# HGRN2 diagonal and levels of 1 to 16 tokens as column-tiled products in chunks of 32, and 512-column value projections

## The chip, the cores and the metric

The kernel runs on one core of a Trainium2 chip. The core has a matrix engine (TensorE, "PE" in the profile, with its weight loads listed apart as "PEld"), an elementwise engine (VectorE, "DVE"), an activation engine (ScalarE, "ACT"), a general engine (GpSimd, "POOL") and a queue engine (SyncE, "SP") that starts transfers. SBUF is the on-chip memory; PSUM, into which TensorE writes, has eight banks, each of 512 fp32 numbers for each of 128 partitions. The metric is the device time of one execution in microseconds, as the median over runs.

## The reference

One decoder layer over 512 tokens of width 1024, in fp32. A single projection of x gives the inputs of two token mixers. The first is an mLSTM with 4 heads of 512. The second is HGRN2 with 8 heads, key width 128 and value width 128. Both results are normalised, gated, projected and merged; two layer norms and a SwiGLU network follow. The part around the change is HGRN2, here for one head, with log_f the log of a forget gate, k = 1 - f and chunks of 16 tokens:

```python
a = jnp.cumsum(lfc, axis=2)
rel = jnp.where(causal, a[:, :, :, None, :] - a[:, :, None, :, :], -jnp.inf)
scores = jnp.einsum('bhtk,bhtsk,bhsk->bhts', qc, jnp.exp(rel), kc)
o = (jnp.einsum('bhts,bhsv->bhtv', scores, vc)
     + jnp.einsum('bhtk,bhkv->bhtv', qc * jnp.exp(a), state))
```

The score of query token t and key token s is a sum over 128 features of q, k and the product of all forget gates between s and t. The values vc are a plain projection, x times columns of W_in plus a bias; so are the values of the mLSTM.

## The kernel before

**Products.** Every large product is done by `mm3` (lines 83 to 86): both operands are split in a rounded high part and a remainder (`split`, line 89: a cast on ScalarE and a subtraction on VectorE), and three matmuls add high x high, high x low and low x high into one PSUM bank. HGRN2's own products multiply plain fp32 operands; the trace shows each of these as two weight loads and two matmuls.

**Weights.** `fetch` brings 512 KB of a weight matrix into one of five raw buffers (`wraw`, started on SP's queue) and splits it into one of three pairs `whi` and `wlo`. `proj_sub` (line 141) makes a projection with features in the partitions: 128 weight columns are stationary and 512 tokens move, 8 x 3 matmuls of 512 columns. `natural_proj` (line 156) makes one with tokens in the partitions: a 128 x 128 block of x is stationary and weight columns move, 256 at a time. It makes 4 token tiles x 8 x 3 = 96 matmuls of 256 columns, with one fetch for each half of the contraction, into two PSUM banks with two token tiles in each.

**Order.** `tick()` is called after each projection; `defer(n, fn)` puts a piece of other work behind n further ticks (half steps exist). So the attention, the HGRN2 levels and the norms are laid between projections. A planner of the framework then orders each engine's instructions by its own costs, keeping to priorities and dependencies.

**mLSTM stage.** Four heads in turn. Each has eight feature projections (keys, queries), then two value projections of 256 columns (`natural_proj` and `values`; the first head has one of its halves done ahead, with the gates), then four output gates. `attend` multiplies weights and values; a column of ones beside the first 256 value columns gives the denominator. PSUM holds three `pp` banks for projections, three score banks and two `px` banks.

**HGRN2 stage.** Four pairs of heads. `h_units` (line 527) makes for each pair the projections f (two; they give the gates and K), Q (two), the values (one `natural_proj` with the bias load `vb`), and the output gates (two): eight ticks. `h_chain` (line 721) then lays the pair's scores into the ticks of the next pair's projections, for the last pair into those of the merge gates. PSUM holds three `pp` and five `px` banks.

The scores are built up by levels. A tile `ad` holds, for both heads and four blocks of 128 tokens, the scores inside a block.

- The diagonal and the levels of 1 and 2 tokens go a direct way (`h_direct_0` to `h_direct_3`). VectorE multiplies K and Q element by element (`h_terms`, 128 x 512, five times for a pair), the product is split, and a matmul with a matrix of ones as the stationary operand sums it over the 128 features (`h_sum`, line 579, two matmuls of 512 columns each, ten for a pair). A predicated copy with a mask puts the sums in place in `ad`.
- A level of hs tokens (`h_level`, line 637) multiplies K of the first half of each group of 2 hs tokens with Q of the second half. Between levels `h_advance` (lines 592, 593, 596) multiplies the gates into K and Q, so each level's products come after the advance of the level before.
- Levels 4 and 8 (line 656) take whole blocks: 128 stationary columns of K, 64 moving columns of Q, eight products for a pair. Only a part of what they give is used; `h_place` (line 604) picks it with a mask from 512 columns.
- Levels 16 and 32 (line 647) take only the groups. With `tile_position=(0, s0)` a product uses a strip of the array's columns, s0 being 0, 32, 64 or 96 for level 16 (32 products of 16 stationary and 16 moving columns) and 0 or 64 for level 32 (16 products of 32 and 32).
- Levels 64, 128 and 256 (lines 661, 667, 673) follow, and `h_out` (line 689) multiplies the scores with the values and normalises.

The direct steps are due after 0, 1, 2 and 3 ticks, the levels after 3.5, 4, 4.5, 5, 5.5, 6 and 6.5, the outputs after 7 and 7.5.

Of the kernel before, what the change touches and what calls it, by code (L numbers as in the profile page):

```python
# [15 lines left out]
P = 128  # L16
# [20 lines left out]
def tile_hybrid_trunk(  # L37
# [79 lines left out]
    ones_r = cst.tile([P, P], FR, name="ones")  # L117
    ones = ones_r.bitcast(F32)
# [30 lines left out]
    def natural_half(outs, s_, wh, wl, shared=True):  # L149
        for t in range(NT):  # L150
            for k in range(4):
                kx = 4 * s_ + k
                mm3(outs[t], xh[:, kx, t * P:(t + 1) * P], xl[:, kx, t * P:(t + 1) * P], wh[:, k], wl[:, k],
                    kx == 0 and not (shared and t % 2), kx == KD - 1, skip_group_check=True)

    def natural_proj(off):
        vps = [psum(pp, "pp", (P, 2, 256)) for _ in range(2)]
        outs = [vps[t // 2][:, t % 2] for t in range(NT)]
        for s_ in range(2):
            natural_half(outs, s_, *fetch(win[s_ * 512:(s_ + 1) * 512, off:off + 256], 4, 256))  # L160
            if s_ == 0:
                tick()
        return vps
# [57 lines left out]
    for s_ in range(2):  # L221
        natural_half(vps0, s_, *wv[s_], shared=False)
# [156 lines left out]
    def values(h, u2, vps, vt_):  # L379
        vh, vl, vb = vt_  # L380
        us2 = slice(u2 * 256, (u2 + 1) * 256)
        vs2 = slice(u2 * 258, u2 * 258 + 256)
        for g in range(2):
            vt = mp.tile([P, 2, 256], F32, tag="w32", name="vt", bufs=4)
            nc.vector.tensor_add(vt, vps[g], vb[:, None, us2].to_broadcast([P, 2, 256]))
            split(vt, vh[:, 2 * g:2 * g + 2, vs2], vl[:, 2 * g:2 * g + 2, vs2])

    def value_tiles(h):
        vh = mp.tile([P, NT, 514], FR, tag="vh", name="vh")
        vl = mp.tile([P, NT, 514], FR, tag="vl", name="vl")  # L390
        nc.vector.memset(vh[:, :, 256:258].bitcast(F32), 1.0)
        nc.vector.memset(vl[:, :, 256:258].bitcast(F32), 0.0)
        vb = mp.tile([P, MD], F32, tag="vb", name="vb")
        nc.sync.dma_start(vb, b_in[:, O_MV + h * MD:O_MV + (h + 1) * MD].to_broadcast([P, MD]))
        return vh, vl, vb

    def attend(h, tiles, wth, wtl, vh, vl, hn):
        for i in tiles:
            nps = [psum(px, "px", (P, 258)), psum(sp, f"s{i % 3}", (P, 256))]
            for e, vs in enumerate((slice(0, 258), slice(258, 514))):  # L400
# [3 lines left out]
            den = nps[0][:, 256:257]  # L404
# [50 lines left out]
    for h in range(MH):  # L455
# [57 lines left out]
    for key, gs_, w in (((1, 0), 2, 1), ((2, 0), 4, 2), ((2, 1), 4, 2), (4, 8, 4), (8, 16, 8)):  # L513
        a, n = (key[1], 1) if isinstance(key, tuple) else (0, w)
        m = hp_.tile([P, P // gs_, w], F32, name=f"mask{gs_}{a}")
        nc.gpsimd.memset(m, 1.0)
        for sg_, base in ((1, -a), (-1, a + n - 1)):
            nc.gpsimd.affine_select(m, m, pattern=[[-gs_ * sg_, P // gs_], [0, w]],
                                    compare_op=OP.is_ge, fill=0.0, base=base, channel_multiplier=sg_)
        masks[key] = m  # L520
    ads = []
    for i in range(2):
        ad = hp_.tile([P, 8, P], F32, name=f"ad{i}")
        nc.gpsimd.memset(ad, 0.0)
        ads.append(ad)

    def h_units(pr):

        st = dict(pr=pr, ad=ads[pr % 2])
        for name in ("f", "K", "Q", "og"):  # L530
            st[name] = hp_.tile([P, 2, T], F32, tag=name, name=name, bufs=2)
        st["v"] = hp_.tile([P, NT, 256], F32, tag="v", name="v", bufs=2)
        st["tot"] = hp_.tile([P, 1024], F32, tag="tot", name="tot", bufs=1)
        f, K, Q, og, v = (st[k] for k in ("f", "K", "Q", "og", "v"))
# [17 lines left out]
        vb = hp_.tile([P, 256], F32, tag="vb", name="vb")  # L552
        nc.sync.dma_start(vb, b_in[:, O_HI + pr * 256:O_HI + (pr + 1) * 256].to_broadcast([P, 256]))
        vps = natural_proj(O_HI + pr * 256)
        for g in range(2):
            nc.vector.tensor_add(v[:, 2 * g:2 * g + 2], vps[g], vb[:, None, :].to_broadcast([P, 2, 256]))
        tick()
# [7 lines left out]

    def h_terms(in0, in1, shape):

        e = hp_.tile(shape, F32, tag="e", name="e", bufs=2)
        eh = hp_.tile(shape, FR, tag="eh", name="eh", bufs=2)
        el = hp_.tile(shape, FR, tag="el", name="el", bufs=2)  # L570
        nc.vector.tensor_mul(e, in0, in1)
        split(e, eh, el)
        return eh, el

    def h_sum(parts, n):

        ps = psum(px, "px", (P, T // n, n))
        for i, part in enumerate(parts):
            nc.tensor.matmul(ps.rearrange("p j n -> p (j n)"), ones_r, part.rearrange("p a b -> p (a b)"),  # L579
                             start=(i == 0), stop=(i == 1))  # L580
        return ps
# [18 lines left out]
    def h_place(st, ps, gs_, w, key):  # L600

        dst = st["ad"].rearrange("p j (g k) -> p j g k", k=gs_)[:, :, :, gs_ - w:]
        msk = masks[key].bitcast(U32)[:, None].to_broadcast([P, 8, P // gs_, w])
        nc.vector.copy_predicated(dst, msk, ps.rearrange("p j (g k) -> p j g k", k=w))

    def h_direct_0(st):
        K, Q, f = st["K"], st["Q"], st["f"]
        st["e"] = [h_terms(K[:, c:c + 1], Q[:, c:c + 1], [P, 1, T]) for c in range(2)]
        nc.vector.tensor_mul(Q, Q, f)
        st["cur"] = f.rearrange("p c t -> p (c t)")  # L610
# [4 lines left out]
    def h_direct_1(st):  # L615
        ad = st["ad"]
        dpss = [h_sum(parts, P) for parts in st["e"]]
        qv, kv = h_halves(st, 1)
        st["e"] = h_terms(kv[:, :, 0], qv[:, :, 1], [P, T, 1])
        h_advance(st, 1)  # L620
        for c in range(2):
            nc.vector.copy_predicated(ad[:, 4 * c:4 * c + 4], ident.bitcast(U32)[:, None, :].to_broadcast([P, NT, P]),
                                      dpss[c])

    def h_direct_2(st):
        ps = h_sum(st["e"], 64)
        qv, kv = h_halves(st, 2)
        st["e"] = [h_terms(kv[:, :, 0, a:a + 1].to_broadcast([P, 256, 2]), qv[:, :, 1], [P, 256, 2]) for a in range(2)]
        h_advance(st, 2)
        h_place(st, ps, 2, 1, (1, 0))  # L630

    def h_direct_3(st):
        pss = [h_sum(parts, 64) for parts in st["e"]]
        for a in range(2):
            h_place(st, pss[a], 4, 2, (2, a))

    def h_level(st, hs):

        K, Q, ad = st["K"], st["Q"], st["ad"]
        if hs in (16, 32):  # L640

            lps = psum(px, "px", (P, 8, 64))
            for c in range(2):
                for j in range(NT):
                    for g in range(64 // hs):
                        s0 = 2 * hs * g
                        nc.tensor.matmul(lps[s0:s0 + hs, 4 * c + j, hs * g:hs * (g + 1)],
                                         K[:, c, j * P + s0:j * P + s0 + hs], Q[:, c, j * P + s0 + hs:j * P + s0 + 2 * hs],
                                         start=True, stop=True, tile_position=(0, s0))
        elif hs < 64:  # L650
            lps = psum(px, "px", (P, 8, 64))
            for c in range(2):
                for j in range(NT):
                    js = slice(j * P, (j + 1) * P)
                    mov = Q[:, c, js].rearrange("p (g two h) -> p g two h", two=2, h=hs)[:, :, 1]
                    nc.tensor.matmul(lps[:, 4 * c + j], K[:, c, js], mov, start=True, stop=True)  # L656
# [21 lines left out]
        if hs < 16:  # L678
            h_place(st, lps, 2 * hs, hs, hs)
        elif hs < 64:  # L680
            for g in range(64 // hs):
                rows_ = slice(2 * hs * g, 2 * hs * g + hs)
                nc.scalar.copy(ad[rows_, :, 2 * hs * g + hs:2 * hs * (g + 1)], lps[rows_, :, hs * g:hs * (g + 1)])
# [5 lines left out]
    def h_out(st, c):  # L689
# [3 lines left out]
        vc = lambda j: st["v"][:, j, c * P:(c + 1) * P]  # L693
# [47 lines left out]
    sgb2 = [hp_.tile([P, 2, T], F32, tag=tag, name="sgb", bufs=2) for tag in ("f", "K", "Q", "v")]  # L741
# [184 lines left out]
```

## Time and profile before

| | |
|---|---|
| median of 3 runs (lowest, highest) | 1326.18 us (1325.97, 1326.56) |
| profiled execution, its own time | 1324.7 us |
| its span, first to last instruction | 1322.9 us |
| mean granted TensorE clock | 0.997 |
| stretch of the span read for the HGRN2 stage | 548 to 820 us |
| bytes moved, share of 16 transfer engines | 141.34 MB, 37.1% |

The page lists busy times, slices, queues, the chain of work that ended last, the costliest groups and the transfers. In the timeline a row has the start and the length in us, the engine, the line of the kernel, the operation, "out<-in" by tile names, stationary rows * columns and the moving operand's size, and xcount. Lengths of matmuls overlap, since the array is a pipeline. In the view of groups the two numbers after the bar are the busy time in us and the mean of one in ns. In the view of stretches a row has the stretch, its length, and for each engine the busy us and the number of instructions: TensorE, weight loads, VectorE, ScalarE, GpSimd; at the end stand the granted clock, the share of the transfer engines and GB/s. With a filter such a row has only the engine asked for; instructions still running from before are counted too.

### The profile page before, as it was taken

The page shows a single profiled execution, that of the slowest core. Times are in us where ns is not written, and L with a number is a line of the kernel's source. Part 1 is how long each engine was busy: PE and PEld are TensorE (multiplying, and loading weights), DVE is VectorE, ACT ScalarE, POOL GpSimd, SP SyncE. Part 2 cuts the span into 40 slices and gives each one's busy share as a digit, 9 for nine tenths or more (in the row PEclk, how much of TensorE's full clock was granted, in tenths as well). Part 3 has the DMA queues.
Part 4 walks back from the last instruction along what each step waited for, and adds up shares of the span by engine and source line. Part 5 has one row for each costly group of instructions (what it writes and reads, how often), then busy time and mean ns, then how long its engine had stood idle before and what let it go on. Part 6 is the DMA issues. An engine that isn't in the chain of part 4 may idle for free.

```text
span 1322.9 us, 17916 instructions
## 1 busy us (share of the span) xinstructions
PE 1306.4 (99%) x7279; PEld 1124.9 (85%) x7279; DVE 752.2 (57%) x1140; ACT 536.4 (41%) x811; POOL 41.1 (3%) x78
## 2 busy tenths in 40 slices
PE   8999999999999999999999999999999999999997
PEld 7788889888988898889898988887898888888885
DVE  5774656466556654458686764255765433334565
ACT  5764553444343533323434333333773222223332
POOL 0000000000000001000000000000000000000001
PEclk9999999999999999999999999999999999999999
DMA  8322333223322323333232322336664343335672
GB/s 236 80 72 80 91 86 90 78 80 96 88 80 80 96 80 84 96 84 84 64 85 65 79 64 65 96 95 204 200 180 127 97 132 96 96 96 168 195 225 81
DMA packets 189426, 141.34 MB, mean 107 GB/s; under 512 B 5728, under 2 KB 178592, under 8 KB 189344
## 3 DMA queue, kind: packets, MB, share of 16 engines
q1 hardware_dynamic: 188288, 140.17, 37.1%
q8 instruction: 57, 0.93, 0.3%
q14 instruction: 25, 0.20, 0.1%
q10 hardware_dynamic: 1056, 0.03, 0.0%
HBM read 138.09 MB, written 2.10 MB: 106 GB/s over the span
## 4 chain that ended last, share of the span: by engine, by line
PE 94%; DVE 2%; ACT 2%; issue 1%; DMA 1%; POOL 0%; SPq 0%; DVEq 0%; POOLq 0%; ACTq 0%
PE pp L84 19%; PE pp L86 19%; PE pp L85 19%; PE pf L86 9%; PE pf L84 9%; PE pf L85 9%; PE px L702 1%; PE s L85 1%; PE s L86 1%; PE px L656 1%; PE s L84 1%; PE px L579 1%; ACT xt L825 1%; DMA xn<-in_x_dram 1%; PE px L424 1%
## 5 line engine op out<-in xcount | busy, mean ns | idle before, releaser
L89 ACT CAST whi<-wraw 128x1024 fp32r<-128x1024 f32 x246 | 258.1, 1050 | 593.1 <-PE pp L85 253.4
L89 DVE TENSOR_TENSOR wlo<-wraw,whi 128x1024 fp32r<-128x1024 f32 x246 | 300.5, 1223 | 270.5 <-ACT whi L89 267.3
L84 PE MATMUL pp<-xh,whi 128*128 128x512 f32 x704 | 278.0, 395 | 0.0
L86 PE MATMUL pp<-xh,wlo 128*128 128x512 f32 x704 | 275.7, 392 | 0.0
L85 PE MATMUL pp<-xl,whi 128*128 128x512 f32 x704 | 275.2, 391 | 0.0
L86 PEld LDWEIGHTS pp<-xh,wlo 128*128 128x128 f32 x704 | 132.6, 188 | 28.2 <-issue 0.4
L84 PEld LDWEIGHTS pp<-xh,whi 128*128 128x128 f32 x704 | 132.7, 188 | 27.4 <-issue 1.0
L85 PEld LDWEIGHTS pp<-xl,whi 128*128 128x128 f32 x704 | 132.6, 188 | 26.4
L86 PE MATMUL pf<-x1h,wlo 128*128 128x512 f32 (+1 forms) x416 | 148.4, 357 | 0.7 <-DVE wlo L89 0.7
L84 PE MATMUL pf<-x1h,whi 128*128 128x512 f32 (+1 forms) x416 | 148.4, 357 | 0.0
L85 PE MATMUL pf<-x1l,whi 128*128 128x512 f32 (+1 forms) x416 | 148.3, 356 | 0.0
L84 PE MATMUL pp<-whi,xh 128*128 128x256 f32 x352 | 100.7, 286 | 0.0
L86 PE MATMUL pp<-whi,xl 128*128 128x256 f32 x352 | 99.8, 284 | 0.0
L85 PE MATMUL pp<-wlo,xh 128*128 128x256 f32 x352 | 99.6, 283 | 0.0
L86 PEld LDWEIGHTS pf<-x1h,wlo 128*128 128x128 f32 x416 | 78.6, 189 | 12.2 <-DVE wlo L89 0.9
L85 PEld LDWEIGHTS pf<-x1l,whi 128*128 128x128 f32 x416 | 78.6, 189 | 11.3
L84 PEld LDWEIGHTS pf<-x1h,whi 128*128 128x128 f32 x416 | 78.6, 189 | 11.1
L357 DVE SCALAR_TENSOR_TENSOR y<-u,cols,y 128x512 f32<-128x512 f32 x96 | 71.8, 749 | 6.1 <-ACT y L355 2.6
L85 PE MATMUL pf<-wlo,g 128*128 128x512 f32 x176 | 68.6, 390 | 0.0
L86 PE MATMUL pf<-whi,g 128*128 128x512 f32 x176 | 68.5, 389 | 0.0
L84 PE MATMUL pf<-whi,g 128*128 128x512 f32 x176 | 68.4, 389 | 0.0
L84 PEld LDWEIGHTS pp<-whi,xh 128*128 128x128 f32 x352 | 67.4, 192 | 0.2
(253 smaller groups left out, 1916.0 us busy)
## 6 DMA issues: line engine op xcount, KB each, us to landing
wraw<-in_w_in_dram SPq DMA_DIRECT2D x110, 512.0 KB, 3.9
wraw<-in_w_ffn_down_dram SPq DMA_DIRECT2D x44, 512.0 KB, 4.2
wraw<-in_w_ffn_gate_dram SPq DMA_DIRECT2D x26, 512.0 KB, 4.0
wraw<-in_w_ffn_up_dram SPq DMA_DIRECT2D x26, 512.0 KB, 3.9
wraw<-in_w_proj_a_dram SPq DMA_DIRECT2D x16, 512.0 KB, 3.5
wraw<-in_w_out_dram SPq DMA_DIRECT2D x16, 512.0 KB, 3.7
wraw<-in_w_proj_b_dram SPq DMA_DIRECT2D x8, 512.0 KB, 3.8
xn<-in_x_dram SPq DMA_DIRECT2D x4, 512.0 KB, 4.9
```

Source lines behind the costliest of these rows:

```text
L84: nc.tensor.matmul(ps, lh, rh, start=start, stop=False, **kw)
L85: nc.tensor.matmul(ps, lh, rl, start=False, stop=False, **kw)
L86: nc.tensor.matmul(ps, ll, rh, start=False, stop=stop, **kw)
L89: return nc.scalar.copy(hi, src), nc.vector.tensor_sub(lo, src, hi.bitcast(F32))
L357: nc.vector.scalar_tensor_tensor(y, u[:, tap:tap + T], cwcol(tap, ch), y, op0=OP.mult, op1=OP.add)
L424: nc.tensor.transpose(tps[:, i * P:(i + 1) * P], hn[:, i, c * P:(c + 1) * P], ident)
L579: nc.tensor.matmul(ps.rearrange("p j n -> p (j n)"), ones_r, part.rearrange("p a b -> p (a b)"), start=(i == 0), stop=(i == 1))
L656: nc.tensor.matmul(lps[:, 4 * c + j], K[:, c, js], mov, start=True, stop=True)
L702: nc.tensor.matmul(ops[:, i], at, vc(j), start=(e == 0), stop=(e == len(terms) - 1))
L825: nc.scalar.activation(xt[:, k], tps[:, k], AF.Identity, bias=b1col(kk), scale=g1col(kk))
```

## The change

**Wide projections.** A new `natural_wide` projects 512 columns at once: four fetches, each a quarter of the contraction by 512 columns, 4 x 8 x 3 = 96 matmuls of 512 columns into four banks (three `pp` and one `px`), with three ticks inside. Heads 1 to 3 of the mLSTM use it in place of two `natural_proj`; the first head keeps its narrow half. The denominator's column of ones moves from behind the first 256 value columns to the end. For HGRN2, the values of pairs 0 and 1 are projected together at the start of pair 1's units, those of pairs 2 and 3 at the start of pair 2's. Their bias load takes a buffer of the tag "sg", and the value tiles have three buffers.

**Scores inside chunks of 32.** The direct way with its products, splits and sums by ones is gone. `h_chunks` makes, for each 32 tokens, a product with 32 stationary columns of K in the column strip of that chunk: strips 0, 32, 64 and 96, K and Q of the same chunk, 32 products for a pair. The diagonal moves all 32 columns of Q, the levels 1, 2, 4, 8 and 16 the 16 columns of the second halves. Predicated copies with new masks put the results into a tile `adc` of 32 columns for each chunk; after level 16 four ScalarE copies bring it into `ad`. Level 32 makes the same products as before. GpSimd builds the masks with more instructions, in buffers of the tag "sg".

**Due times.** With six ticks in pairs 0 and 3 and ten in pairs 1 and 2, the diagonal is due at once, levels 1 to 256 after 0.5, 1.25, 2, 2.75, 3.5, 4, 4.5, 5 and 5.5, the outputs after 6 and 6.5.

```diff
-    def natural_half(outs, s_, wh, wl, shared=True):
+    def natural_part(outs, k0, wh, wl, shared=False):
+
         for t in range(NT):
-            for k in range(4):
-                kx = 4 * s_ + k
+            for k in range(wh.shape[1]):
+                kx = k0 + k
                 mm3(outs[t], xh[:, kx, t * P:(t + 1) * P], xl[:, kx, t * P:(t + 1) * P], wh[:, k], wl[:, k],
                     kx == 0 and not (shared and t % 2), kx == KD - 1, skip_group_check=True)
...
+    def natural_wide(off):
+
+        vps = [psum(*((pp, "pp") if t < 3 else (px, "px"))) for t in range(NT)]
+        for s_ in range(4):
+            natural_part(vps, 2 * s_, *fetch(win[s_ * 256:(s_ + 1) * 256, off:off + 512], 2, 512))
+            if s_ < 3:
                 tick()
         return vps
...
+            for t in range(NT):
+                vt = mp.tile([P, MD], F32, tag="w32", name="vt", bufs=4)
+                nc.vector.tensor_add(vt, vps[t], vb)
+                split(vt, vh[:, t, 0:512], vl[:, t, 0:512])
...
-        for u2 in range(1 if h == 0 else 0, 2):
-            vps = natural_proj(O_MV + h * MD + u2 * 256)
-            values(h, u2, vps, vt_)
-            tick()
+        values(natural_proj(O_MV + 256) if h == 0 else natural_wide(O_MV + h * MD), vt_)
+        tick()
...
+    for hs in (1, 2, 4, 8, 16):
+        ng = 64 // hs
+        m4 = hp_.tile([P, 4, ng // 4, hs], F32, tag="sg", name="m4", bufs=2)
+        m4v = m4.rearrange("p c g h -> p (c g) h")
+        nc.gpsimd.memset(m4, 1.0)
+        for sg_, base in ((1, 0), (-1, hs - 1)):
+            nc.gpsimd.affine_select(m4v, m4v, pattern=[[-2 * hs * sg_, ng], [0, hs]],
                                     compare_op=OP.is_ge, fill=0.0, base=base, channel_multiplier=sg_)
...
+        nc.gpsimd.tensor_add(m4[:, 0], m4[:, 0], m4[:, 1])
+        nc.gpsimd.tensor_add(m4[:, 2], m4[:, 2], m4[:, 3])
+        nc.gpsimd.tensor_add(masks[hs], m4[:, 0], m4[:, 2])
...
+        if pr in (1, 2):
+            lo = 0 if pr == 1 else 2
+            vb = hp_.tile([P, 512], F32, tag="sg", name="vb", bufs=2)
+            nc.sync.dma_start(vb, b_in[:, O_HI + lo * 256:O_HI + (lo + 2) * 256].to_broadcast([P, 512]))
+            vps = natural_wide(O_HI + lo * 256)
+            for q in range(2):
+                vs_[lo + q] = hp_.tile([P, NT, 256], F32, tag="v", name="v", bufs=3)
+            for t in range(NT):
+                for q in range(2):
+                    qs = slice(q * 256, (q + 1) * 256)
+                    nc.vector.tensor_add(vs_[lo + q][:, t], vps[t][:, qs], vb[:, qs])
+            tick()
...
+    def h_chunks(st, n, targets):
+
+        ps = psum(px, "px", (P, 8, n))
+        for c in range(2):
+            for j in range(NT):
+                for g in range(4):
+                    cs = slice(j * P + 32 * g, j * P + 32 * g + 32)
+                    nc.tensor.matmul(ps[32 * g:32 * g + 32, 4 * c + j], st["K"][:, c, cs], targets(st["Q"][:, c, cs]),
+                                     start=True, stop=True, tile_position=(0, 32 * g))
+        return ps
+
+    def h_diagonal(st):
+        Q, f = st["Q"], st["f"]
+        ps = h_chunks(st, 32, lambda q: q)
         nc.vector.tensor_mul(Q, Q, f)
+        nc.vector.copy_predicated(st["adc"], same.bitcast(U32)[:, None].to_broadcast([P, 8, 32]), ps)
...
+        if hs < 32:
+            lps = h_chunks(st, 16, lambda q: q.rearrange("p (g two h) -> p g two h", two=2, h=hs)[:, :, 1])
...
+        if hs < 32:
+            adc = st["adc"]
+            nc.vector.copy_predicated(adc.rearrange("p j (g two h) -> p j g two h", two=2, h=hs)[:, :, :, 1],
+                                      masks[hs].bitcast(U32)[:, None].to_broadcast([P, 8, 16 // hs, hs]),
+                                      lps.rearrange("p j (g h) -> p j g h", h=hs))
+            if hs == 16:
+                for g in range(4):
+                    rows_ = slice(32 * g, 32 * g + 32)
+                    nc.scalar.copy(ad[rows_, :, 32 * g:32 * g + 32], adc[rows_])
...
-        steps = [(0, h_direct_0), (1, h_direct_1), (2, h_direct_2), (3, h_direct_3)]
+        steps = [(0, h_diagonal)]
         steps += [(t, lambda st, hs=hs: h_level(st, hs)) for t, hs in
-                  ((3.5, 4), (4, 8), (4.5, 16), (5, 32), (5.5, 64), (6, 128), (6.5, 256))]
-        steps += [(7 + 0.5 * c, lambda st, c=c: h_out(st, c)) for c in range(2)]
+                  ((0.5, 1), (1.25, 2), (2, 4), (2.75, 8), (3.5, 16), (4, 32), (4.5, 64), (5, 128), (5.5, 256))]
+        steps += [(6 + 0.5 * c, lambda st, c=c: h_out(st, c)) for c in range(2)]
```

More of the change, by code (lines that the diff above doesn't have):

```diff
@@ L116, in tile_hybrid_trunk @@
     tri = cst.tile([P, P], F32, name="tri")
-    ones_r = cst.tile([P, P], FR, name="ones")
-    ones = ones_r.bitcast(F32)
+    ones = cst.tile([P, P], F32, name="ones")
     nc.gpsimd.memset(ones, 1.0)
@@ L221, in tile_hybrid_trunk @@
     for s_ in range(2):
-        natural_half(vps0, s_, *wv[s_], shared=False)
+        natural_part(vps0, 4 * s_, *wv[s_])
     cols = cst.tile([P, 3 * P], F32, name="cols")
@@ L377, in weights, with values @@
             split(w32[:, :n], wth[:, o:o + n], wtl[:, o:o + n])
-    def values(h, u2, vps, vt_):
+    def values(vps, vt_):
         vh, vl, vb = vt_
[L381 to L386, printed above, removed]
+        if len(vps) == 2:
+            for g in range(2):
+                vt = mp.tile([P, 2, 256], F32, tag="w32", name="vt", bufs=4)
+                nc.vector.tensor_add(vt, vps[g], vb[:, None, 256:512].to_broadcast([P, 2, 256]))
+                split(vt, vh[:, 2 * g:2 * g + 2, 256:512], vl[:, 2 * g:2 * g + 2, 256:512])
+        else:
+            for t in range(NT):
+                vt = mp.tile([P, MD], F32, tag="w32", name="vt", bufs=4)
+                nc.vector.tensor_add(vt, vps[t], vb)
+                split(vt, vh[:, t, 0:512], vl[:, t, 0:512])
     def value_tiles(h):
@@ L390, in value_tiles @@
         vl = mp.tile([P, NT, 514], FR, tag="vl", name="vl")
-        nc.vector.memset(vh[:, :, 256:258].bitcast(F32), 1.0)
-        nc.vector.memset(vl[:, :, 256:258].bitcast(F32), 0.0)
+        nc.vector.memset(vh[:, :, 512:514].bitcast(F32), 1.0)
+        nc.vector.memset(vl[:, :, 512:514].bitcast(F32), 0.0)
         vb = mp.tile([P, MD], F32, tag="vb", name="vb")
@@ L398, in attend @@
         for i in tiles:
-            nps = [psum(px, "px", (P, 258)), psum(sp, f"s{i % 3}", (P, 256))]
-            for e, vs in enumerate((slice(0, 258), slice(258, 514))):
+            nps = [psum(px, "px", (P, 256)), psum(sp, f"s{i % 3}", (P, 258))]
+            for e, vs in enumerate((slice(0, 256), slice(256, 514))):
                 for j in range(i + 1):
@@ L512, in tile_hybrid_trunk @@
     masks = {}
[L513 to L518, printed above, removed]
-                                    compare_op=OP.is_ge, fill=0.0, base=base, channel_multiplier=sg_)
-        masks[key] = m
+    for hs in (1, 2, 4, 8, 16):
[5 more added lines that the diff above has]
+            nc.gpsimd.affine_select(m4v, m4v, pattern=[[-2 * hs * sg_, ng], [0, hs]],
+                                    compare_op=OP.is_ge, fill=0.0, base=base, channel_multiplier=sg_)
+        masks[hs] = hp_.tile([P, ng // 4, hs], F32, name=f"mask{hs}")
+        nc.gpsimd.tensor_add(m4[:, 0], m4[:, 0], m4[:, 1])
+        nc.gpsimd.tensor_add(m4[:, 2], m4[:, 2], m4[:, 3])
+        nc.gpsimd.tensor_add(masks[hs], m4[:, 0], m4[:, 2])
+    same = hp_.tile([P, 32], F32, name="same")
+    nc.gpsimd.memset(same, 0.0)
+    for g in range(4):
+        nc.gpsimd.affine_select(same, same, pattern=[[-1, 32]], compare_op=OP.not_equal, fill=1.0,
+                                base=-32 * g, channel_multiplier=1)
     ads = []
@@ L524, in tile_hybrid_trunk @@
         nc.gpsimd.memset(ad, 0.0)
-        ads.append(ad)
+        adc = hp_.tile([P, 8, 32], F32, name=f"adc{i}")
+        nc.gpsimd.memset(adc, 0.0)
+        ads.append((ad, adc))
+    vs_ = {}
     def h_units(pr):
-        st = dict(pr=pr, ad=ads[pr % 2])
+        st = dict(pr=pr, ad=ads[pr % 2][0], adc=ads[pr % 2][1])
         for name in ("f", "K", "Q", "og"):
             st[name] = hp_.tile([P, 2, T], F32, tag=name, name=name, bufs=2)
-        st["v"] = hp_.tile([P, NT, 256], F32, tag="v", name="v", bufs=2)
         st["tot"] = hp_.tile([P, 1024], F32, tag="tot", name="tot", bufs=1)
-        f, K, Q, og, v = (st[k] for k in ("f", "K", "Q", "og", "v"))
+        f, K, Q, og = (st[k] for k in ("f", "K", "Q", "og"))
+        if pr in (1, 2):
[9 more added lines that the diff above has]
+                    nc.vector.tensor_add(vs_[lo + q][:, t], vps[t][:, qs], vb[:, qs])
+            tick()
         for c in range(2):
@@ L551, in h_units @@
             tick()
[L552 to L557, printed above, removed]
         for c in range(2):
@@ L564, in h_units @@
         return st
[L566 to L581, printed above, removed]
     def h_halves(st, hs):
@@ L598, in h_advance @@
             st["toff"] += nb
[L600 to L608, printed above, removed]
+    def h_chunks(st, n, targets):
[10 more added lines that the diff above has]
+        ps = h_chunks(st, 32, lambda q: q)
         nc.vector.tensor_mul(Q, Q, f)
+        nc.vector.copy_predicated(st["adc"], same.bitcast(U32)[:, None].to_broadcast([P, 8, 32]), ps)
         st["cur"] = f.rearrange("p c t -> p (c t)")
@@ L613, in h_direct_0 @@
         st["a2"] = hp_.tile([P, 2, 2, 256], F32, tag="a2", name="a2", bufs=1)
[L615 to L635, printed above, removed]
     def h_level(st, hs):
         K, Q, ad = st["K"], st["Q"], st["ad"]
-        if hs in (16, 32):
+        if hs < 32:
+            lps = h_chunks(st, 16, lambda q: q.rearrange("p (g two h) -> p g two h", two=2, h=hs)[:, :, 1])
+        elif hs == 32:
             lps = psum(px, "px", (P, 8, 64))
@@ L644, in h_level @@
                 for j in range(NT):
[L645 to L656, printed above, removed]
+                    for s0 in (0, 64):
+                        src = j * P + s0
+                        nc.tensor.matmul(lps[s0:s0 + 32, 4 * c + j, s0 // 2:s0 // 2 + 32], K[:, c, src:src + 32],
+                                         Q[:, c, src + 32:src + 64], start=True, stop=True, tile_position=(0, s0))
         elif hs == 64:
@@ L677, in h_level @@
         h_advance(st, hs)
[L678 to L683, printed above, removed]
+        if hs < 32:
[4 more added lines that the diff above has]
+            if hs == 16:
+                for g in range(4):
+                    rows_ = slice(32 * g, 32 * g + 32)
+                    nc.scalar.copy(ad[rows_, :, 32 * g:32 * g + 32], adc[rows_])
+        elif hs == 32:
+            for s0 in (0, 64):
+                nc.scalar.copy(ad[s0:s0 + 32, :, s0 + 32:s0 + 64], lps[s0:s0 + 32, :, s0 // 2:s0 // 2 + 32])
         elif hs == 64:
@@ L692, in h_out @@
         ops = psum(px, "px", (P, NT, P))
-        vc = lambda j: st["v"][:, j, c * P:(c + 1) * P]
+        vc = lambda j: vs_[st["pr"]][:, j, c * P:(c + 1) * P]
         for i in range(NT):
@@ L740, in tile_hybrid_trunk @@
         nc.vector.tensor_mul(accn(n), accn(n), sg)
-    sgb2 = [hp_.tile([P, 2, T], F32, tag=tag, name="sgb", bufs=2) for tag in ("f", "K", "Q", "v")]
+    sgb2 = [hp_.tile([P, 2, T], F32, tag=tag, name="sgb", bufs=n_) for tag, n_ in (("f", 2), ("K", 2), ("Q", 2), ("v", 3))]
     sgbs = [sgb2[n // 2][:, n % 2] for n in range(KD)]
```

5 lines of the change are left out of this document (3 added, 2 removed).

## The prediction

> **What bounds the kernel now.** I read the page first: the span, the busy times and the chain of waits.
>
> ```profile
> span 1322.9 us, 17916 instructions
> PE 1306.4 (99%) x7279; PEld 1124.9 (85%) x7279; DVE 752.2 (57%) x1140; ACT 536.4 (41%) x811; POOL 41.1 (3%) x78
> PE 94%; DVE 2%; ACT 2%; issue 1%; DMA 1%; POOL 0%; SPq 0%; DVEq 0%; POOLq 0%; ACTq 0%
> ```
>
> TensorE carries 94% of the chain. Busy alone could hide bubbles, so I asked the busy times by stretches for the HGRN2 stage, and VectorE's groups by form.
>
> ```profile
> 548.00:820.00 272.00, 272.00 (x1941) 238.08 (x1940) 179.65 (x263) 99.08 (x197) 6.06 (x6) 1.00 0.30 78
> ```
> ```profile
> L592 DVE TENSOR_TENSOR Q<-Q,tot 128x512 f32<-128x512 f32 x28 | 19.2, 686 | 10.1 <-PE px L656 6.4 <-PE px L667 1.9 <-PE px L647 1.8
> ```
>
> TensorE (first number after the length) is busy 272.00 of 272.00 us at full clock, VectorE 180 (third), ScalarE 99 (fourth). So what the change takes from VectorE and ScalarE (per pair of heads five products with their splits, and larger predicated copies) is worth nothing: TensorE hides it. The time is TensorE's, and the change is priced in TensorE time. A matmul's shown duration includes its pipeline, so I use distances between starts, from the timeline of TensorE.
>
> ```profile
> 579.79 0.39 PE L84 MATMUL pp<-xh,whi 128*128 128x512 f32 x1
> ...
> 588.40 0.39 PE L86 MATMUL pp<-xh,wlo 128*128 128x512 f32 x1
> 588.63 0.40 PE L579 MATMUL px<-eh,ones 128*128 128x512 f32 x1
> ...
> 589.56 0.39 PE L84 MATMUL pp<-xh,whi 128*128 128x512 f32 x1
> ...
> 595.03 0.40 PE L579 MATMUL px<-eh,ones 128*128 128x512 f32 x1
> ...
> 595.50 0.39 PE L84 MATMUL pp<-xh,whi 128*128 128x512 f32 x1
> ...
> 600.96 0.40 PE L579 MATMUL px<-eh,ones 128*128 128x512 f32 x1
> ...
> 601.90 0.39 PE L84 MATMUL pp<-xh,whi 128*128 128x512 f32 x1
> ...
> 609.50 0.28 PE L84 MATMUL pp<-whi,xh 128*128 128x256 f32 x1
> ...
> 612.26 0.28 PE L86 MATMUL pp<-whi,xl 128*128 128x256 f32 x1
> 612.38 1.90 PE L656 MATMUL px<-Q,K 128*128 128x64 f32 x16
> 614.09 0.36 PE L84 MATMUL pp<-whi,xh 128*128 128x256 f32 x1
> 614.29 0.28 PE L85 MATMUL pp<-wlo,xh 128*128 128x256 f32 x1
> ...
> 616.56 0.28 PE L86 MATMUL pp<-whi,xl 128*128 128x256 f32 x1
> 616.77 0.70 PE L647 MATMUL px<-Q,K 128*16 128x16 f32 x64
> ...
> 617.62 0.28 PE L85 MATMUL pp<-wlo,xh 128*128 128x256 f32 x1
> ...
> 619.05 0.28 PE L85 MATMUL pp<-wlo,xh 128*128 128x256 f32 x1
> 619.30 0.70 PE L647 MATMUL px<-Q,K 128*32 128x32 f32 x32
> ...
> 620.15 0.28 PE L84 MATMUL pp<-whi,xh 128*128 128x256 f32 x1
> ```
>
> From 579.79 to 588.40 lie 38 steps: 226.6 ns for 512 columns. From 609.50 to 612.26 lie 23: 120.0 ns for 256. Two halves take 240.0 ns, one whole 226.6: each matmul pays about 13 ns beside its columns.
>
> **Wide projections.** Heads 1 to 3 have two half projections of 96 matmuls each (576), the four HGRN2 pairs one each (384): 960 matmuls of 256 columns, 115.2 us, become 480 of 512, 108.8 us. Saved: 6.4 us. Head 0 keeps its narrow half.
>
> **Removed in HGRN2, per pair of heads.** The ten matmuls with the matrix of ones: 0.93 + 0.47 + 0.94 = 2.34 us. The full-array levels of 4 and 8 tokens: where a projection matmul should have followed at 612.38 with the next at 612.50, the next came at 614.29, so 1.79 us each. The level of 16: 616.68 should have been the start after 616.56, and the matmul after that stands at 617.62 in place of 616.80: 0.82 us. The level of 32 in the same way costs 0.86 us (620.15 against 619.29), and stays, with the same 16 products. Over four pairs: 4 x (2.34 + 2 x 1.79 + 0.82) = 27.0 us.
>
> **Added.** Six groups per pair (the diagonal, levels 1 to 16), 24 in all. Each has 32 products with 32 stationary columns in four column tiles of the array. An fp32 product is two weight loads and two matmuls in the trace (16 products in the level of 32 are x32), so a group is x64. No row shows 32 columns in four tiles; two rows lie near. The level of 16 has the same x64 in the same four tiles, with 16 stationary columns: 0.82 us, the lower end. The level of 32 has the same columns in two tiles, x32. For the rate I read the weight loads.
>
> ```profile
> 616.77 0.59 PEld L647 LDWEIGHTS px<-Q,K 128*16 128x16 f32 x64
> ```
> ```profile
> 619.27 0.62 PEld L647 LDWEIGHTS px<-Q,K 128*32 128x32 f32 x32
> ```
> ```profile
> 624.18 1.01 PEld L661 LDWEIGHTS px<-Q,K 128*64 128x64 f32 x16
> ```
> ```profile
> L661 PEld LDWEIGHTS px<-Q,K 128*64 128x64 f32 x64 | 4.0, 138 | 0.8 <-PE pp L85 0.4
> L647 PEld LDWEIGHTS px<-Q,K 128*32 128x32 f32 x128 | 2.4, 112 | 0.8 <-issue 0.4
> L647 PEld LDWEIGHTS px<-Q,K 128*16 128x16 f32 x256 | 2.4, 93 | 0.8 <-PE pp L85 0.4
> ```
>
> Extent less one load, by the number of steps: 58 ns between loads for 64 columns in one tile, 16.4 ns for 32 in two tiles, 7.9 ns for 16 in four. Per column that is 0.91, 0.51 and 0.49 ns. Going from one tile to two halves it; going from two to four does nothing more. The counts of loads begun by short stretches show why:
>
> ```profile
> 619.26:619.29 0.03, 0.02 (x1) 1.00 0.00 0
> 619.29:619.32 0.03, 0.03 (x3) 1.00 0.00 0
> 619.32:619.35 0.03, 0.03 (x5) 1.00 0.00 0
> ```
> ```profile
> 616.76:616.79 0.03, 0.02 (x4) 1.00 0.00 0
> 616.79:616.82 0.03, 0.03 (x9) 1.00 0.00 0
> ```
>
> A load lasts 112 ns, so these counts add up what has begun: one load alone, then two more each 30 ns. I read it so: the first load of a product goes alone, the second waits for its own tile to come free, and since loads start in order, only the next tile's first load can go beside it. Two per turn, then, however many tiles there are, and a group of x64 takes 0.86 + 32 x 0.0164 = 1.38 us. Against this stands that 16-column loads begin five in 30 ns, more than two tiles at 32 columns' pace, scaled, would give (four). I take 1.38, because the stationary columns are the same; 24 x 1.38 = 33.1 us. A level moves 16 columns and not 32, but the full-array level moves 64 against 128 stationary columns and still takes 1.70 us for 16, so the load sets the pace.
>
> The Trainium skill, TensorEngine Tiling (Array Packing), section Theoretical Speedup, promises up to four times for operands of 32 or fewer columns; by that the sum would be the second case below. The step from two tiles to four in this trace, 0.51 to 0.49 ns per column, does not show it.
>
> **The sum.** -6.4 - 27.0 + 33.1 = -0.3 us. The profiled execution took 1324.7 us, so 1324.4; the median of the runs shown stands 1.5 us higher, at 1326.18, so the forecast is 1325.9 us.
>
> **At nothing, with the cover.** The wide projection holds all three pp banks and one px. At its start the third bank must have been emptied; twelve matmuls, 2.7 us, come first. At its end the next projection needs the first bank, whose last matmul lies 18 matmuls, 4.1 us, back; VectorE's additions there must have been done.
>
> ```profile
> 583.16 1.05 ACT L89 CAST whi<-wraw 128x1024 fp32r<-128x1024 f32 x1 [3.76 <-PE pp L85]
> 584.12 0.68 ACT L562 ACTIVATE og<-pp,cols 128x512 f32<-128x512 f32 x1
> ```
> ```profile
> L89 DVE TENSOR_TENSOR wlo<-wraw,whi 128x1024 fp32r<-128x1024 f32 x44 | 53.9, 1225 | 44.0 <-ACT whi L89 44.0
> ```
>
> A cast ahead of a gate's sigmoid makes 1.05 + 0.68 = 1.73 us against 2.7; a split ahead of an addition, at the 0.69 us of the multiplications of that size, 1.23 + 0.69 = 1.92 against 4.1. Without the cover each place costs 1 to 2 us. The HGRN2 values' weight loads and bias load move on SP's queue from the middle of every pair to the start of pairs 1 and 2. The bias load now waits for a buffer of the sigmoids and squares, and the weight loads queue behind it; five raw buffers, each some 24 matmuls or 5.4 us of work, lie between, so only a wait over some 20 us would reach TensorE. GpSimd makes the new masks, in buffers that the sigmoid of the first Q needs next:
>
> ```profile
> 524.76 3.49 POOL L518 TENSOR_SCALAR_AFFINE_SELECT mask<-mask 128x64 f32<-128x64 f32 x6
> ```
> ```profile
> 556.26 0.68 ACT L549 ACTIVATE sg<-pp,cols 128x512 f32<-128x512 f32 x1
> ```
>
> Thirty instructions at 0.58 us are 17 us, and 31 lie between; were they twice as long, ScalarE would wait some 4 us once. Moving the ones column of the mLSTM values from one bank to the other changes no count.
>
> **The rivals.**
>
> Four tiles really side by side (chance 0.25). Then a group costs 0.82 us, as the level of 16 with its x64: 24 x 0.82 = 19.7, the sum is -13.7, and the time 1312.5 us. If only the levels, which move 16 columns, gain it and the diagonal doesn't: 20 x 0.82 + 4 x 1.38 = 21.9, -11.5, 1314.7 us. For it: five loads in 30 ns. Against it: the cost per column.
>
> The banks bind (0.12), the case on the other side. Five wide projections, each waiting 1 us at its start for the third bank and 1 us at its end for the first: 10 us on the forecast, 1335.9 us. It decides once VectorE's queue at the end of a wide projection is longer than 4.1 us, or ScalarE's at its start than 2.7. Against it: today's evacuations are done in 1.7 to 1.9 us.
>
> Loads one at a time (0.04). 0.91 ns per column from the row of one tile is 29 ns for 32 columns; 64 of them are 1.86 us, with 0.33 us of entry and exit (0.86 - 32 x 0.0164) 2.19; 24 x 2.19 = 52.6 and the time 1345.4 us. The Trainium skill, TensorE: Matmul & The Clock Gate, Part 3, The mechanism, says that a weight load overlaps running matmuls only where the row group differs; here every product uses all rows. The trace does not agree: loads of 32 columns begin 16.4 ns apart, not 29.
>
> The planner leaves both levels of one tick (2 and 4) with nothing between (0.03). Then TensorE stands for the two 0.69 us multiplications of the first: at least 1.4 us, over four pairs 5.6, 1331.5 us. Against it: the stage has no such gap today, though the levels of 4 and 8 share a tick.
>
> **How the numbers follow.** The forecast, two loads per turn, has 0.56, with 1324.0 to 1328.5 as its own range. A measurement of this kernel can tell about 0.2%, 2.65 us, from no change. Faster by more than that: the second case and a little of the first, 0.28. Slower: the banks, the single loads, the planner and the first case's upper end, 0.20. The rest, 0.52, is no change. The range from 1312.0 to 1329.0 holds the forecast and the case of four tiles and leaves out most of the slower ones.
>
> **What would show it.** In the profile after, the groups of levels 1 to 16 as x64 with 128*32: weight loads spanning 1.1 us mean two per turn, 0.6 us four. The wide projections at 227 ns a matmul, without a gap before the third bank's first or the next projection's first matmul. Matmuls in all: 7279 - 480 - 40 - 128 - 256 + 1536 = 7911. I am wrong if TensorE shows idle time in the HGRN2 stage, or if a group of x64 takes neither 0.8 nor 1.4 us.

## The result, and the profile after

The changed kernel takes 1315.48 us (median of 5 runs, 1313.78 to 1318.76) against 1325.97 us for the kernel before on the same chip (5 runs). The ratio is 0.9922, with a 95% interval of 0.9909 to 0.9934: faster by 0.8%, about 10 us. The forecast was 1325.9 us, no change. The time lies inside the range from 1312.0 to 1329.0, near the case of four tiles side by side, which had a chance of 0.25.

First the page of the changed kernel: span, busy times and chain of waits.

```profile
span 1313.9 us, 19136 instructions
PE 1297.1 (99%) x7911; PEld 1091.0 (83%) x7911; DVE 709.9 (54%) x1104; ACT 528.5 (40%) x791; POOL 45.5 (3%) x100
PE 97%; DVE 1%; ACT 1%; DMA 1%; issue 0%; POOL 0%; SPq 0%; DVEq 0%; POOLq 0%
```

The count of matmuls, 7911, is the one worked out ahead. TensorE still carries the chain. The span is 9.0 us shorter. To see where, I take the starts at the borders of the stages from the timeline of TensorE: the last matmul of the first value projection, the first projection matmul behind the last head's gates, the first matmul of the output projection, and the last matmul. The kernel before:

```profile
22.91 0.28 PE L86 MATMUL px<-wvh,xl 128*128 128x264 f32 x1
...
511.70 0.48 PE L84 MATMUL pp<-xh,whi 128*128 128x512 f32 x1
...
904.41 0.47 PE L84 MATMUL pf<-whi,mxh 128*128 128x512 f32 x1 [0.88 <-DVE sgb L751]
...
1314.18 0.39 PE L86 MATMUL pf<-whi,g 128*128 128x512 f32 x1
```

The changed kernel:

```profile
24.96 0.28 PE L86 MATMUL px<-wvh,xl 128*128 128x264 f32 x1
...
510.04 0.48 PE L84 MATMUL pp<-xh,whi 128*128 128x512 f32 x1
...
895.25 0.47 PE L84 MATMUL pf<-whi,mxh 128*128 128x512 f32 x1 [0.87 <-DVE sgb L747]
...
1305.03 0.39 PE L86 MATMUL pf<-whi,g 128*128 128x512 f32 x1
```

| stretch | before, us | after, us | difference | from the prediction's terms |
|---|---|---|---|---|
| start, to the first value projection's end | 22.91 | 24.96 | +2.05 | 0 |
| mLSTM | 488.79 | 485.08 | -3.71 | -3.9 |
| HGRN2 and merge | 392.71 | 385.21 | -7.50 | +3.5 |
| rest, to the last matmul | 409.77 | 409.78 | 0.0 | 0 |

The two microseconds at the start are chance: the same kernel, profiled again below, ends this projection at 23.14. The first transposes of x start 0.4 us later here, and TensorE's first instructions stay slow for longer: groups of four transposes follow each other every 0.86 us until 12.9 us, where in the kernel before they do so every 0.47 us from 9.2 us on. The HGRN2 stage is what the forecast missed: 11 us better than its terms. Around one group of level 1, in the timeline of TensorE:

```profile
569.77 0.39 PE L86 MATMUL pp<-xh,wlo 128*128 128x512 f32 x1
570.09 0.76 PE L620 MATMUL px<-Q,K 128*32 128x32 f32 x64
570.78 0.51 PE L84 MATMUL pp<-whi,xh 128*128 128x512 f32 x1
571.12 0.39 PE L85 MATMUL pp<-wlo,xh 128*128 128x512 f32 x1
...
576.11 0.39 PE L86 MATMUL px<-whi,xl 128*128 128x512 f32 x1
576.43 0.74 PE L620 MATMUL px<-Q,K 128*32 128x16 f32 x64
577.09 0.50 PE L84 MATMUL pp<-whi,xh 128*128 128x512 f32 x1
577.43 0.39 PE L85 MATMUL pp<-wlo,xh 128*128 128x512 f32 x1
```

The first group is the diagonal, the second level 1. Without the diagonal the matmul shown at 571.12 would have stood at 570.22, two steps of 227 ns behind 569.77: it costs 0.90 us. Without level 1 the one at 577.43 would have stood at 576.56: 0.87 us. The forecast took 1.38 for both. The weight loads of level 1, their form, and the loads begun by short stretches:

```profile
576.42 0.64 PEld L620 LDWEIGHTS px<-Q,K 128*32 128x32 f32 x64 [0.35 <-issue]
```
```profile
L620 PEld LDWEIGHTS px<-Q,K 128*32 128x32 f32 x1536 | 15.4, 110 | 8.1 <-issue 4.8 <-PE pp L85 2.5 <-DVE adc L670 0.4
```
```profile
576.42:576.45 0.03, 0.03 (x4) 1.00 0.00 0
576.45:576.48 0.03, 0.03 (x8) 1.00 0.00 0
576.48:576.51 0.03, 0.03 (x12) 1.00 0.00 0
```

A load lasts 110 ns, so the counts add up: four loads begin in each 30 ns, where the level of 32 before the change, with the same 32 columns in two strips, began two. From first to last start, (0.64 - 0.11) / 63 = 8.4 ns a load. The span of 0.64 us is the sign that the prediction gave for four loads per turn. What waits of TensorE are left:

```profile
PE px L209 <- DMA xn<-in_x_dram: 6.0, 2, 5.0
PE pf L84 <- DVE sgb L747: 0.9, 1, 0.9
PE pf L86 <- DVE wlo L89: 0.7, 1, 0.7
PE px L329 <- DVE mrow L317: 0.5, 1, 0.5
PE px L336 <- issue: 0.2, 1, 0.2
```

None is at a wide projection. The one of 0.9 us stands at the very end of the stretch of HGRN2 and merge, as it did before (0.88); none is inside.

### The profile page after: what moved, and what is told of

Its sections match the earlier page's. It is cut to its first block, busy times and chain, and to the rows that moved or that the text cites. A ratio compares the mean times of both kernels' runs of the same rounds, so it can differ in the third digit from the quotient of the medians.

```text
span 1313.9 us, 19136 instructions
## 1 busy us (share of the span) xinstructions
PE 1297.1 (99%) x7911; PEld 1091.0 (83%) x7911; DVE 709.9 (54%) x1104; ACT 528.5 (40%) x791; POOL 45.5 (3%) x100
## 4 chain that ended last, share of the span: by engine, by line
PE 97%; DVE 1%; ACT 1%; DMA 1%; issue 0%; POOL 0%; SPq 0%; DVEq 0%; POOLq 0%
PE pp L84 19%; PE pp L85 18%; PE pp L86 18%; PE pf L84 10%; PE pf L85 10%; PE pf L86 10%; PE px L698 1%; PE px L620 1%; PE px L84 1%; PE px L85 1%; PE px L86 1%; PE s L86 1%; PE s L85 1%; PE s L84 1%; DMA xn<-in_x_dram 1%; PE px L438 1%
## 5 line engine op out<-in xcount | busy, mean ns | idle before, releaser
L84 PEld LDWEIGHTS pp<-xh,whi 128*128 128x128 f32 x704 | 132.5, 188 | 27.4 <-issue 1.0
L84 PEld LDWEIGHTS pf<-x1h,whi 128*128 128x128 f32 x416 | 78.6, 189 | 11.3
L85 PEld LDWEIGHTS pf<-x1l,whi 128*128 128x128 f32 x416 | 78.6, 189 | 11.3
L84 PE MATMUL pp<-whi,xh 128*128 128x512 f32 (+1 forms) x152 | 57.1, 375 | 0.0
L85 PE MATMUL pp<-wlo,xh 128*128 128x512 f32 (+1 forms) x152 | 56.1, 369 | 0.0
L86 PE MATMUL pp<-whi,xl 128*128 128x512 f32 (+1 forms) x152 | 55.9, 367 | 0.0
L84 PE MATMUL pp<-ht,whi 128*128 128x512 f32 x128 | 50.1, 391 | 0.0
```

The lines of the kernel that those rows point to most:

```text
L84: nc.tensor.matmul(ps, lh, rh, start=start, stop=False, **kw)
L85: nc.tensor.matmul(ps, lh, rl, start=False, stop=False, **kw)
L86: nc.tensor.matmul(ps, ll, rh, start=False, stop=stop, **kw)
```

## The experiments

The theory after the result: a strip of 32 columns starts a load about every 31 ns, as many loads are under way as there are different strips among neighbouring products, and the change gains because the groups fill four strips. The rivals: the pace of 8 to 9 ns is the rate at which instructions are issued, whatever the strips; or the gain comes from elsewhere, the relieved VectorE or the wide projections. Every ratio is to the kernel before, on the same chip.

**The mark.** The changed kernel again, as the mark for the runs below. Of the runs with one time only, the HGRN2 and merge stage is compared, since single times scatter by a microsecond or two. One source of it is in the traces: somewhere between 42 and 66 us, early in mLSTM, some seven matmuls of 512 columns start 427 ns apart and not 227 (in this mark from 60 to 62 us, where the granted clock is 0.50). In the profile of this mark that happens once, in others twice (1.5 us more).

> The changed kernel again, as the mark for the other runs of this call. Ratio to before 0.992 as measured. In its first profile TensorE's first value projection started 1.6 us later than in the profile of before and ended 2.1 us later; if that is chance of the first loads of x, this profile's start differs from it by a microsecond or two in some direction; if the change causes it, the value projection ends again near 25.0 us and not near 22.9.

1315.16 us, ratio 0.9916 (0.9902 to 0.9930). The value projection ends at 23.14 us, 0.2 from the kernel before; in a third profile of the changed kernel, the second mark below, it ends at 25.10. The late start comes and goes with the same kernel: it was chance. mLSTM takes 485.14 us, HGRN2 and merge 385.52.

**Narrow projections again.** Everything else as changed.

```diff
-        values(natural_proj(O_MV + 256) if h == 0 else natural_wide(O_MV + h * MD), vt_)
-        tick()
+        for u2 in range(1 if h == 0 else 0, 2):
+            values(natural_proj(O_MV + h * MD + u2 * 256), vt_, u2)
+            tick()
...
-            vps = natural_wide(O_HI + lo * 256)
+            for q in range(2):
+                vps = natural_proj(O_HI + (lo + q) * 256)
```

> The changed kernel with every value projection narrow again (two of 256 columns in the place of each of 512, at the same places in the order). Theory, 13 ns saved for each of 480 matmuls: 6.4 us slower than the changed kernel, 1.3 us for each of the heads 1 to 3 and 2.6 us in HGRN2. Rival, the wide projections lose part of it at their banks: less than 5 us slower.

1321.27 us, ratio 0.9962 (0.9949 to 0.9974): 6.1 us over the mark in the medians. Border rows of its timeline:

```profile
22.73 0.28 PE L86 MATMUL px<-wvh,xl 128*128 128x264 f32 x1
...
511.54 0.48 PE L84 MATMUL pp<-xh,whi 128*128 128x512 f32 x1
...
898.90 0.47 PE L84 MATMUL pf<-whi,mxh 128*128 128x512 f32 x1 [0.87 <-DVE sgb L747]
```

mLSTM takes 488.81 us, 3.7 over the mark (one slow stretch in each of the two); HGRN2 and merge 387.36, 1.8 over. The wide projections give their 13 ns a matmul, a little less in HGRN2 than the 2.6 us worked out. What is left against the kernel before, 0.38%, is the gain of the groups.

**One strip at a time.** The same products, the eight of one strip one behind the other.

```diff
-        for c in range(2):
-            for j in range(NT):
-                for g in range(4):
+        for g, c, j in [(g, c, j) for g in range(4) for c in range(2) for j in range(NT)]:
```

> The changed kernel with the products of each group in another order: all eight of one strip one behind the other. Theory, a strip takes one load per 31.6 ns and only products in different strips go side by side: 64 x 31.6 ns and 0.35 us of entry and exit, 2.4 us for a group in the place of 0.87, 24 x 1.5 = 36 us slower than the changed kernel. Rival, the pace of 8 to 9 ns is set by the issue of instructions and not by strips: no change.

1343.13 us in its one run, 18 us over the kernel before beside it (1324.86). Its HGRN2 and merge stage takes 412.9 us, 27.4 over the mark's 385.5. The weight loads of one group:

```profile
577.40 1.80 PEld L618 LDWEIGHTS px<-Q,K 128*32 128x32 f32 x64 [0.35 <-issue]
```

(1.80 - 0.11) / 63 = 27 ns a load in the place of 8.4. The number of instructions is the same, so their issue doesn't set the pace; the strips do. It is less than 31 ns, and the stage 27 us and not 36 dearer, because loads go in pairs where one strip's run ends and the next begins. The loads under way inside the first run and where it meets the second:

```profile
577.64:577.67 0.03, 0.03 (x4) 1.00 0.00 0
577.85:577.88 0.03, 0.03 (x8) 1.00 0.00 0
```

Inside a run the loads start 31 to 32 ns apart; only the last three of the 16 loads of a run have one of the next strip's beside them.

**Two strips.** Strips 0 and 1 alternate, then 2 and 3.

```diff
-        for c in range(2):
-            for j in range(NT):
-                for g in range(4):
+        for c, p, j, g in [(c, p, j, g) for c in range(2) for p in (0, 2) for j in range(NT) for g in (p, p + 1)]:
```

> The changed kernel with the strips 0 and 1 alternating for four products each, then 2 and 3. Theory, as many loads under way as strips among neighbours: 15.8 ns a load as in level 32, 1.36 us for a group, 24 x 0.49 = 12 us slower than the changed kernel. Rival, the pace is the issue of instructions: no change.

1318.39 us beside 1324.86 for the kernel before. The stage takes 389.8 us, 4.3 over the mark, not 12.

```profile
574.86 0.82 PEld L618 LDWEIGHTS px<-Q,K 128*32 128x32 f32 x64 [0.35 <-issue]
```

(0.82 - 0.11) / 63 = 11.3 ns. Neither the 15.8 of the theory nor the 8.4 of the rival: the number of strips counts, but where a run in one pair of strips gives way to the other pair, more loads are under way. Inside a run, and at such a place:

```profile
574.95:574.98 0.03, 0.03 (x9) 1.00 0.00 0
575.07:575.10 0.03, 0.03 (x14) 1.00 0.00 0
```

**Runs of two.** Two products of a strip, then two of the next.

```diff
-        for c in range(2):
-            for j in range(NT):
-                for g in range(4):
+        for c, b, g, j in [(c, b, g, j) for c in range(2) for b in (0, 2) for g in range(4) for j in (b, b + 1)]:
```

> The changed kernel with two products of one strip one behind the other, then two of the next strip. Theory, TensorE takes loads out of a window of waiting instructions: the group stays near 0.87 us. Rival, loads start in order: a second product of the same strip holds up the next strip's, about two loads under way, 15.8 ns a load, 1.36 us for a group, 12 us slower.

1317.91 us beside 1324.86. The stage takes 387.7 us, 2.2 over the mark: near the theory (no change), far from the rival's 12.

```profile
576.34 0.73 PEld L618 LDWEIGHTS px<-Q,K 128*32 128x32 f32 x64 [0.35 <-issue]
```

(0.73 - 0.11) / 63 = 9.8 ns. Loads started strictly in order would have to wait behind each of four loads of one strip, well over 15 ns a load. So loads pass others that wait for their strip; with runs of eight products (27 ns) they do so only at the last three loads of a run. That reads as a window of limited length; its length was not measured otherwise. The Trainium skill, TensorE: Matmul & The Clock Gate, Part 3, The mechanism, describes a reorder window that pulls weight loads ahead; these runs agree. It ties this to a row group that does not conflict or to the background weight buffer; here all products use all rows, and a different column strip is enough: four loads in 30 ns.

**Work given back to VectorE and ScalarE.** Five unused products and splits per pair of heads.

```diff
+            nc.vector.tensor_mul(e, st["K"][:, i % 2], st["Q"][:, i % 2])
+            split(e, eh, el)
```

> The changed kernel with five extra products of K and Q per pair of heads, each split, on VectorE and ScalarE, as many as the change took away; nothing uses them. Theory, TensorE hides all of it: within 0.5 us of the changed kernel. Rival, a part of the gain came from the relieved VectorE, since each level waits for the advance before it: slower, at most by 4 x 5 x 1.4 = 27 us, and with waits of TensorE in the HGRN2 stage.

1315.71 us, ratio 0.9917 (0.9903 to 0.9932). Busy times by stretches, the changed kernel first, then this one:

```profile
548.00:812.00 264.00, 264.00 (x2871) 216.85 (x2869) 138.83 (x228) 90.92 (x178) 7.39 (x7) 1.00 0.29 77
```
```profile
548.00:812.00 264.00, 263.29 (x2866) 216.23 (x2865) 162.83 (x268) 101.86 (x197) 7.40 (x7) 1.00 0.29 77
```

VectorE has 24 us more to do, TensorE waits 0.7 us, once, and the time is 0.55 us over the mark's, the stage 0.5 (386.0 us). The wait was of this size and there are no others, so the relief of VectorE and ScalarE is worth about half a microsecond; the prediction put it at nothing.

**Levels 32 and 64 in more strips.** The second head's products go to other strips, and ScalarE copies each head's part back.

```diff
-                        nc.tensor.matmul(lps[s0:s0 + 32, 4 * c + j, s0 // 2:s0 // 2 + 32], K[:, c, src:src + 32],
-                                         Q[:, c, src + 32:src + 64], start=True, stop=True, tile_position=(0, s0))
+                        src, r0 = j * P + s0, s0 + 32 * c
+                        nc.tensor.matmul(lps[r0:r0 + 32, j], K[:, c, src:src + 32],
+                                         Q[:, c, src + 32:src + 64], start=True, stop=True, tile_position=(0, r0))
...
-                    nc.tensor.matmul(lps[0:64, 4 * c + j], K[:, c, j * P:j * P + 64], Q[:, c, j * P + 64:(j + 1) * P],
-                                     start=True, stop=True)
+                    nc.tensor.matmul(lps[64 * c:64 * c + 64, j], K[:, c, j * P:j * P + 64],
+                                     Q[:, c, j * P + 64:(j + 1) * P], start=True, stop=True, tile_position=(0, 64 * c))
```

> The changed kernel with level 32 in four column strips (the second head's products in the strips 32 and 96) and level 64 in two strips of 64. Theory, as many loads under way as there are strips among neighbours: level 32 goes from 16.2 to about 8 ns a load, 0.25 us less for each pair; level 64 from 61.6 to about 31 ns, 0.46 us less; 4 x 0.71 = 2.8 us faster than the changed kernel. Rival, two loads per turn however many strips: level 32 stays, only level 64 gains, 1.8 us.

1314.57 us, ratio 0.9906 (0.9891 to 0.9920): the times can't tell it from the mark's 0.9916. The stage can: 382.7 us against 385.5. Loads of level 32 and of level 64:

```profile
598.46 0.35 PEld L645 LDWEIGHTS px<-Q,K 128*32 128x32 f32 x32 [0.36 <-DVE adc L670]
```
```profile
602.94 0.55 PEld L651 LDWEIGHTS px<-Q,K 128*64 128x64 f32 x16 [0.35 <-issue]
```

In the kernel before the change these took 0.62 and 1.01 us. Less a load's own length of 0.11 and 0.14 us, level 32 goes from 16.4 to 7.7 ns a load and level 64 from 58 to 27: twice the strips, half the time. It was run a second time, beside the next one, with the changed kernel as a mark for both.

> The changed kernel a third time, as the mark for the other two runs of this call. Ratio to before 0.992.

> Level 32 in four strips and level 64 in two, again, since the first time told the two kernels apart in the stage (2.8 us) but not in the times. 2.8 us faster than the changed kernel, ratio to before 0.990.

The mark: 1315.76 us, 0.9919 (0.9904 to 0.9934), its stage 385.5 us. This kernel: 1313.68, 0.9907 (0.9890 to 0.9924), its stage 382.7 us again. The intervals still overlap.

**The diagonal and level 1 with one load.** This goes on top of the edit before, with levels 32 and 64 in more strips. K is the same in the diagonal and level 1, so Q and Q times the gates stand side by side in one tile and move behind each other.

```diff
-        ps = h_chunks(st, 32, lambda q: q)
-        nc.vector.tensor_mul(Q, Q, f)
+        nc.vector.tensor_mul(st["QQ"][:, 1], Q, f)
+        ps = psum(px, "px", (P, 8, 2, 32))
...
+                    nc.tensor.matmul(ps[32 * g:32 * g + 32, 4 * c + j], st["K"][:, c, cs], st["QQ"][:, :, c, cs],
+                                     start=True, stop=True, tile_position=(0, 32 * g))
```

> As the kernel with the levels 32 and 64 in more strips, and besides the diagonal and level 1 in one group: both have the same K, so each load of K serves 64 moving columns, 32 of Q and 32 of Q times the gates. Theory, the moving columns set the pace of a strip now (64 fp32 columns, about 58 ns as in level 64), 14.6 ns a load over four strips, 1.28 us for the group in the place of 0.90 + 0.87: 4 x 0.49 = 2.0 us faster than the kernel without it, 4.8 us faster than the changed kernel, ratio to before 0.988. Rival, moving columns of different strips don't go side by side: 64 x 58 ns, 4.0 us for the group, 9 us slower than the kernel without it.

1310.34 us, ratio 0.9879 (0.9862 to 0.9897): 5.4 us under the mark in the medians, of which the medians give 3.3 to the shared load and the rest to the edit before. Its stage takes 380.4 us, 5.1 under the mark and 2.3 under the kernel without the shared load; 2.0 was expected of it.

```profile
573.14 0.94 PEld L635 LDWEIGHTS px<-Q,K 128*32 128x32 f32 x64 [0.35 <-issue]
```

(0.94 - 0.11) / 63 = 13.2 ns a load with 64 columns moving, against 8.4 with 16 and 8.6 with 32. Moving columns of different strips go side by side too. Per strip this is 4 x 13.2 = 53 ns, near the 58 of level 64 in one strip, which also moves 64 columns: from there on the moving columns, and no longer the stationary ones, seem to set the pace.

## Why the prediction came out as it did

**What bounds the kernel: right.** TensorE is busy 264.00 of 264.00 us in the stage, and work given back to VectorE and ScalarE cost about half a microsecond.

**Wide projections, -6.4 us: right.** Taken back, they cost 6.1 us in the medians, 5.5 in the two stages. The banks' cover held: there is no wait at any of the five.

**Removed in HGRN2, 27.0 us: consistent.** No run took one of the removed groups alone. The rows that were read are of one pair of heads; read over all four pairs of the trace before, the groups cost 26.9. With the measured price of the new ones the stage's sum is -2.6 - 27.0 + 4 x 0.90 + 20 x 0.87 = -8.6 us; measured are -7.5.

**Added, 33.1 us: wrong, and this is the step that failed.** The prediction said that loads start in order, so that "only the next tile's first load can go beside it. Two per turn, then, however many tiles there are". A group measures 0.87 to 0.90 us and not 1.38; the 24 cost 21.0 us. The runs show four loads per turn in four strips, two in two (the level of 32), one inside the runs of one strip, and loads that pass waiting ones. The in-order picture fitted the only row of 32 columns because that row had only two strips. The time fell into the range only because the range was drawn to take in the rival with its chance of 0.25; the forecast itself, no change, missed by 10 us.

The argument by columns, 0.51 against 0.49 ns, was a coincidence. The 16-column loads in four strips came 7.9 ns apart, the 32-column loads in four strips come 8.4 ns apart: the level of 16 already stood near a floor that does not grow with the columns. Read as a rate per column, the floor hid what two more strips had gained. The counts by stretches spoke against it (five loads in 30 ns where two strips, scaled, give four), and I gave that too little weight. The row with the same number of instructions, 0.82 us, was the better neighbour than the row with the same width.

**The rivals.** Four tiles side by side is what happened. With 0.82 us for a group it gave 1312.5; the groups are 0.05 to 0.08 us dearer, 1.3 us in all, which makes 1313.8 on the median's footing. The promise of the Trainium skill, TensorEngine Tiling (Array Packing), section Theoretical Speedup, up to four times, is borne out up to 27 / 8.4 = 3.2 between one strip and four. Loads one at a time did not occur in the order chosen; the run with one strip shows that price nearly, 27 ns a load. The banks and the planner did not bind.

**The missing microsecond in HGRN2.** The first output of pairs 0 and 1 takes 0.24 us longer each in TensorE. In it a weight load waits for ScalarE's copy of the scores of the widest level (line 665):

```profile
613.89 0.52 PEld L698 LDWEIGHTS px<-v,a 128*128 128x128 f32 x4 [0.17 <-ACT a L665]
```

And the projection matmuls next behind an fp32 group start 231 to 236 ns apart, not 227: summed over the stage's distances between 229 and 250 ns, the excess is 0.9 us before and 1.4 us after. Together these are 1.0 us. Neither was tried by itself.

## What to carry to other kernels

Small products with few stationary columns are cheap when neighbours in program order lie in different column strips: order the loops so that the strip changes fastest, and fill all four. A price for a form that the trace doesn't show was better taken here from the row with the same count of instructions in the same tiles than from a rate per column, which hides floors. Where TensorE is busy all the time, count its matmuls and weight loads first; products that share a stationary operand can share its load.

## What the runs showed that I had not expected

Weight loads of fp32 in different column strips run side by side, four in about 30 ns, though all use the same rows of the array; and loads pass others that wait for their strip, over a few products but not over runs of eight. Entering and leaving a tiled group costs about a third of a microsecond whatever is in it (0.87 - 64 x 0.0084 = 0.33, and 0.33 in the level of 32; the other runs lie between 0.31 and 0.39), so few large groups are better than many small ones. What sets the floor near 8 ns a load is open. It is not one pace: by the starts of the single loads, the first 32 of a group of level 1 come 7.6 ns apart (6.1 in the level of 16 before the change), and the last 30, behind a gap, 8.7 (8.6). The gap lies where the first head's products end, and no run tells whether the head or the count of 32 makes it.
